# Expert weights through five buffers: three places of 96 slots, routing values in an idle buffer, buffers in address order

## The chip, the core and the metric

The kernel runs on one core of a Trainium2 chip. A core has five engines that matter here: PE (matmul; its weight loads are listed as PEld), DVE (elementwise work), ACT (activations and copies), POOL (general work) and SP, which mostly issues DMAs. Each engine works through its own list of instructions in order and waits on semaphores that others raise. Sixteen DMA engines move data between HBM and SBUF (the on-chip memory); PE writes its sums to PSUM.

The metric is the device time of one execution in microseconds, the median of several.

## The reference

Two residual layers over 256 tokens of width 1024, in float32. The first is attention of two kinds and a dense SwiGLU; the second is sliding-window attention, a short convolution and, last, eight experts of which each token takes two. Only this last part is touched:

```
logits = (xt @ w_router).astype(float32)          # 256 tokens, 8 experts
top_vals, top_idx = lax.top_k(logits, 2)
top_w = softmax(top_vals)
gates = einsum('nk,nke->ne', top_w, one_hot(top_idx, 8))
y = zeros_like(xt)
for e in range(8):
    y = y + gates[:, e:e+1] * swiglu(xt, w_gate[e], w_up[e], w_down[e])   # 1024 -> 3584 -> 1024
out = rms_norm(h + y, final_norm)
```

`top_k` prefers the smaller index where two logits are equal.

## The kernel before, in words

Up to about 500 us the kernel does everything ahead of the experts: each dense weight comes in as a load of 1 MB (`raw`), is split into a high and a low part (`whi`, `wlo`; ACT, DVE and POOL share this) and used in three products. The last of these weights is `w_out` of the second layer, four pieces: two for the first 512 columns, then two for the others. The stretch between the last pieces holds the routing: `route1` transposes h into the buffer `t.dr[0]` (tile `raw`), `logits` multiplies it with the router, `route2` and `route3` make the norm (DVE, POOL, then ACT writes the scaled `xg`), and `choose` (L929 to L956) ranks each token's eight logits, by counting for each expert how many beat it. The rank gives the mask `mb`, two products give every token's position among its expert's tokens, and `dispatch` and `gather` pick each expert's tokens by a product with a matrix of zeros and ones.

The experts are worked through in eight places. Place 0 always holds expert 0; the other seven experts are sorted by their number of tokens (`arrange`, L959 to L982), and `RANKS` says which of them goes to which place. `CAPS` is the number of slots (rows for tokens) that a place has: 64 or 96. If an expert has more tokens than its place has slots, a second pass with the weights of that expert runs after the first (`rest`, under `tc.If(t.over > 0)`). A place has twelve loads of 3,584 KB from HBM: four of w_gate, four of w_up, four of w_down (`part_in`, L1122, and `part_out`, L1130). A load of w_gate or w_up of a place with 64 slots takes two groups of column tiles on PE for each of four k (`into`, L1140), one with 96 slots three; a load of w_down takes seven steps of y, and with 96 slots seven of yo beside them (`down`, L1186). The order within a place: gate and up for the first half of the hidden units, with the last down loads of the place before between them, then gate, down of the first half, and up for the second half. Work on tokens (dispatch, gather, transposes of hid, scatter into h) is put between these by the list `fill`.

The loads go through five buffers of 28 KB per partition (`raw()`, L135), taken in turn: two from the pool `big`, which is opened early and whose two loads come in pieces during the first layer, and three from the pool `big2`, opened in `experts_open` at the start of the expert part. Its memory is what the parts of the kernel before have left; so the first load into each of the three waits for whoever used that memory last. Here the three loads are sent at once, and SP issues them in this order. From then on every `into` and `down` sends the next load when it has used its own (`weights.send()`), so a load is issued when the load five places ahead of it has been read. SP's list is in order: a load that has to wait holds up those behind it.

PE's order, and for a part of the routing ACT's and DVE's too, is the order in which the code is written (`in_order`). The rest is set by the tile framework, which also adds the waits.

The lines that matter most, in `experts_open` and in `raw`:

```
raw_pools.append((lpool("big2", 3), 3, BIG))
turn[0] = 2
for _ in range(3):
    weights.send()
```

```
n = sum(c for _, c, _ in raw_pools)
i = turn[0] % n
turn[0] += 1
```

## Time and profile before

| | us |
|---|---|
| median of 3 runs | 1336.55 |
| lowest and highest run | 1336.16, 1337.74 |
| the profiled execution | 1339.13 |
| span of the profiled execution | 1337.30 |
| PE busy in the span | 1285.7 |
| DVE, ACT, POOL busy | 373.7, 303.3, 167.3 |

The span runs from the first to the last instruction of one execution. A share of busy time is a mean over stages: up to 500 us the DMA engines move less than 300 GB/s, from 500 us on both PE and the DMA engines are shown as nearly always busy. The clock that PE was granted was 0.984 of full speed over the whole span. In the rows, "x" is a count of instructions; matmuls of float32 appear as two instructions each; a bracket at the end of a row of the timeline gives how long the engine was idle ahead of it and what ended that.

### The profile page before, as it was taken

What the parts mean: (1) busy time and instruction counts of PE and PEld (TensorE: products, weight loads), DVE (VectorE), ACT (ScalarE), POOL (GpSimd) and SP (SyncE); (2) the same over time, 40 slices, a digit from 0 to 9 for tenths busy, and PEclk for the clock granted to TensorE, in tenths of its full rate; (3) what the DMA queues carried; (4) which work ended last, traced back from release to release, by engine and by line L of the source; (5) the groups of instructions that cost most, each with busy time, mean ns of one, the idle gap of its engine ahead of it and who ended that gap; (6) DMA issues with size and microseconds to landing.
All of it is one profiled execution on the core that took longest, in us unless ns stands there. A gap on an engine that the chain in (4) does not pass through costs nothing.

```text
span 1337.3 us, 23873 instructions
## 1 busy us (share of the span) xinstructions
PE 1285.7 (96%) x10713; PEld 697.2 (52%) x10713; DVE 373.7 (28%) x697; ACT 303.3 (23%) x495; POOL 167.3 (13%) x116
## 2 busy tenths in 40 slices
PE   7999899999999999999999898999999999999995
PEld 6876678888879783433333332433333343333332
DVE  7666445445465831001012001000201200100202
ACT  6565444443344621100000100100000010000001
POOL 3311344334434110000000000000000000000000
PEclk9999899999999999999999999999999999999997
DMA  8620785555555249999999999999999999999993
GB/s 272 207 93 1 294 287 189 182 177 178 187 166 181 95 183 433 415 427 431 422 426 430 416 428 425 424 432 386 397 384 399 429 420 428 434 419 426 427 426 134
DMA packets 75758, 431.71 MB, mean 323 GB/s; under 512 B 3676, under 2 KB 7792, under 8 KB 71424
## 3 DMA queue, kind: packets, MB, share of 16 engines
q1 hardware_dynamic: 75088, 428.48, 80.0%
q8 instruction: 86, 1.41, 0.4%
q0 software_dynamic: 416, 1.10, 0.2%
q10 hardware_dynamic: 144, 0.52, 0.1%
q14 instruction: 24, 0.20, 0.0%
HBM read 429.04 MB, written 1.05 MB: 322 GB/s over the span
## 4 chain that ended last, share of the span: by engine, by line
PE 82%; DMA 11%; DVE 2%; ACT 1%; POOL 1%; issue 0%; POOLq 0%; ACTq 0%
PE mm L1150 32%; PE y L1193 11%; PE mm L201 8%; PE mm L202 8%; PE mm L203 8%; DMA big<-in_l_w_up_dram 8%; PE yo L1197 4%; DMA big<-in_l_w_down_dram 2%; PE tt L1177 1%; PE tt L1101 1%; PE ww L373 1%; PE ww L203 1%; PE ww L201 1%; PE ww L202 1%; PE mm L416 1%; DMA raw<-in_l_w_gate_dram 1%
## 5 line engine op out<-in xcount | busy, mean ns | idle before, releaser
L1150 PE MATMUL mm<-big,g 128*32 128x448 f32 x5120 | 495.1, 544 | 11.6 <-DMA big<-in_l_w_up_dram 10.5
L1150 PEld LDWEIGHTS mm<-big,g 128*32 128x32 f32 x5120 | 165.4, 111 | 320.1 <-issue 297.5
L1193 PE MATMUL y<-big,ehT 128*32 128x512 f32 x1792 | 215.2, 593 | 0.4 <-DMA big<-in_l_w_down_dram 0.4
L164 POOL TENSOR_TENSOR wlo<-raw,whi 128x288 fp32r<-128x288 f32 (+6 forms) x74 | 154.5, 2089 | 287.2 <-ACT whi L160 266.5
L162 DVE TENSOR_TENSOR wlo<-raw,whi 128x1760 fp32r<-128x1760 f32 (+6 forms) x74 | 143.0, 1934 | 134.0 <-ACT whi L160 133.7
L160 ACT ACTIVATE whi<-raw 128x2048 fp32r<-128x2048 f32 (+4 forms) x74 | 134.4, 1816 | 154.2 <-PE mm L203 82.3
L201 PE MATMUL mm<-whi,xh 128*128 128x512 f32 (+3 forms) x352 | 139.1, 396 | 1.7 <-ACT whi L160 0.9
L202 PE MATMUL mm<-wlo,xh 128*128 128x512 f32 (+3 forms) x352 | 137.2, 390 | 3.0 <-POOL wlo L164 3.0
L203 PE MATMUL mm<-whi,xl 128*128 128x512 f32 (+3 forms) x352 | 137.0, 390 | 1.4 <-DVE xl L290 1.3
L1178 ACT ACTIVATE ehT<-tt 128x512 f32<-128x512 f32 (+1 forms) x32 | 15.6, 487 | 520.3 <-PE tt L1177 520.2
L1164 DVE TENSOR_TENSOR hid<-hid,mm 128x448 f32<-128x448 f32 x40 | 24.9, 621 | 306.8 <-PE mm L1150 303.7
L1294 POOL TENSOR_TENSOR fs<-fs,nhalf 128x1 f32<-128x1 f32 x2 | 1.1, 548 | 830.3 <-DVE fs L1293 830.3
L1193 PEld LDWEIGHTS y<-big,ehT 128*32 128x32 f32 x1792 | 56.9, 110 | 81.5 <-issue 62.9
L201 PEld LDWEIGHTS mm<-whi,xh 128*128 128x128 f32 x352 | 67.7, 192 | 17.6 <-issue 1.8
L202 PEld LDWEIGHTS mm<-wlo,xh 128*128 128x128 f32 x352 | 67.7, 192 | 16.9 <-POOL wlo L164 3.3
L203 PEld LDWEIGHTS mm<-whi,xl 128*128 128x128 f32 x352 | 67.3, 191 | 16.8 <-DVE xl L290 3.1
L1197 PE MATMUL yo<-big,ehT 128*32 128x256 f32 x896 | 68.9, 379 | 0.0
L1197 PEld LDWEIGHTS yo<-big,ehT 128*32 128x32 f32 x896 | 29.1, 110 | 67.0 <-issue 65.3
L201 PE MATMUL mm<-xh,whi 128*128 128x256 f32 x160 | 46.6, 291 | 0.0
L202 PE MATMUL mm<-xl,whi 128*128 128x256 f32 x160 | 45.2, 283 | 0.0
L203 PE MATMUL mm<-xh,wlo 128*128 128x256 f32 x160 | 45.2, 283 | 0.0
L1180 DVE COPY ehT<-tt 128x384 f32<-128x384 f32 x16 | 8.9, 558 | 124.0 <-PE tt L1177 124.0
(310 smaller groups left out, 1048.0 us busy)
## 6 DMA issues: line engine op xcount, KB each, us to landing
big<-in_l_w_up_dram SPq DMA_DIRECT2D x32, 3584.0 KB, 26.8
big<-in_l_w_down_dram SPq DMA_DIRECT2D x31, 3584.0 KB, 26.2
big<-in_l_w_gate_dram SPq DMA_DIRECT2D x30, 3584.0 KB, 24.7
raw<-in_l_w_in_dram SPq DMA_DIRECT2D x15, 1024.0 KB, 5.0
raw<-in_l_w_gate_dram SPq DMA_DIRECT2D x14, 1024.0 KB, 5.0
raw<-in_l_w_up_dram SPq DMA_DIRECT2D x14, 1024.0 KB, 5.0
raw<-in_l_w_down_dram SPq DMA_DIRECT2D x14, 1024.0 KB, 4.9
raw<-in_l_w_out_dram SPq DMA_DIRECT2D x8, 1024.0 KB, 5.0
```

Source lines behind the costliest of these rows:

```text
L160: A.activation(hi, v, AF.Copy)
L162: V.tensor_tensor(lo[:, :, :m], v[:, :, :m], hi[:, :, :m].bitcast(F32), op=OP.subtract)
L164: G.tensor_tensor(lo[:, :, m:], v[:, :, m:], hi[:, :, m:].bitcast(F32), op=OP.subtract)
L201: T.matmul(ps, l[0], r[0], start=first, stop=False, **kw)
L202: T.matmul(ps, l[0], r[1], start=False, stop=False, **kw)
L203: T.matmul(ps, l[1], r[0], start=False, stop=last, **kw)
L373: T.matmul(p[:, i, Q], q[i][:, qs], k[i][:, 0:n], start=True, stop=bias is None)
L1150: T.matmul(ps[key][j][i * O:(i + 1) * O], x[:, k0 + k, g * O:(g + 1) * O], w[:, k, c:c + CH], **at)
L1164: V.tensor_tensor(x[:, g], x[:, g], ps["u"][g], op=OP.mult)
L1178: copy = V.tensor_copy if j0 else lambda a_, b_: A.activation(a_, b_, AF.Copy)
L1193: T.matmul(t.y[c * O:(c + 1) * O], x[:, (2 * i + c % 2) * O:(2 * i + c % 2 + 1) * O], w[:, j, c // 2 * 512:(c // 2 + 1) * 512], **at)
L1197: T.matmul(t.yo[c * O:(c + 1) * O], x[:, (4 + i) * O:(5 + i) * O], w[:, j, c * 256:(c + 1) * 256], **at)
```

## The change

`CAPS` and `RANKS` are changed, so that the places with 96 slots are 1, 3 and 5 in place of 1, 3, 4 and 6. The three experts with most tokens (of the seven sorted ones) get 96 slots, where four did; the fourth goes to place 2, with 64. The groups of places that are gathered together are (0), (1, 2), (3, 4), (5, 6), (7), where they were (0), (1, 2), (3), (4, 5), (6, 7).

The pool `big2` with three buffers becomes three pools `big2`, `big3`, `big4` with one buffer each, used in this order.

The small values of the routing (`lg`, `gt`, `rank`, `far`, `pos`, `count` and those of `arrange` and `gates`) move from the pool `rp` into the first 528 numbers per partition of `t.dr[0]`, the buffer that held h transposed for the router; `rp` gets smaller by as much, and the pools that are opened above it start lower.

In `choose` the two comparisons, the product with `lower` and the sum become a subtraction and one comparison with a constant `least`, which is minus the smallest normal number where the other expert has the smaller index, and zero elsewhere. `gt` is float32 now, and was bf16.

```diff
-CAPS = (64, 96, 64, 96, 96, 64, 96, 64)
-RANKS = (0, 4, 1, 2, 5, 3, 6)
+CAPS = (64, 96, 64, 96, 64, 96, 64, 64)
+RANKS = (0, 3, 1, 4, 2, 5, 6)
...
+    least = consts.tile([128, NE, NE], F32, name="least")
...
+        V.tensor_scalar(least, lower, -2.0 ** -126, None, op0=OP.mult)
...
+    def tmp(*shape):
+        n = math.prod(shape)
+        v = t.dr[0][:, t.used:t.used + n]
+        t.used += n
+        if len(shape) == 1:
+            return v
+        names = "abc"[:len(shape)]
+        return v.rearrange(f"p ({' '.join(names)}) -> p {' '.join(names)}", **dict(zip(names, shape)))
...
     def choose():
         rp = t.rp
-        t.lg = rp.tile([128, NB, NE], F32, name="lg")
+        t.used = 0
+        t.lg = tmp(NB, NE)
         V.tensor_copy(t.lg, t.pl)
-        gt = rp.tile([128, NB, NE, NE], BF, name="gt")
-        eq = rp.tile([128, NB, NE, NE], BF, name="eq")
-        t.rank = rp.tile([128, NB, NE], F32, name="rank")
+        gt = tmp(NB * NE, NE).rearrange("p (b e) f -> p b e f", b=NB)
+        t.rank = tmp(NB, NE)
...
-        V.tensor_tensor(eq, other, own, op=OP.is_equal)
-        V.tensor_tensor(gt, other, own, op=OP.is_gt)
-        V.tensor_tensor(eq, eq, lower[:, None, :, :].to_broadcast([128, NB, NE, NE]), op=OP.mult)
-        V.tensor_tensor(gt, gt, eq, op=OP.add)
+        V.tensor_tensor(gt, other, own, op=OP.subtract)
+        V.tensor_tensor(gt, gt, least[:, None, :, :].to_broadcast([128, NB, NE, NE]), op=OP.is_gt)
         V.tensor_reduce(t.rank, gt, axis=AX.X, op=OP.add)
...
-        raw_pools.append((lpool("big2", 3), 3, BIG))
+        raw_pools.extend((lpool(f"big{i}"), 1, BIG) for i in range(2, 5))
...
-    mine = experts((0,) * NE, CAPS, ((0,), (1, 2), (3,), (4, 5), (6, 7)), [do(experts_open)],
+    mine = experts((0,) * NE, CAPS, ((0,), (1, 2), (3, 4), (5, 6), (7,)), [do(experts_open)],
```

What this does to the lists of the engines, at three places.

SP, from the last load of `w_out` to the third load that waits for PE's use of a buffer. The names: `big` is an expert load, `most` the expert numbers that SP reads; a bracket lists the semaphores on which a row waits, by the engine or DMA lane that raises them. Before:

```order
L149 DMA raw<-in_l_w_out_dram 128x4x512 [waits DMAHW1_49,DVE_49,Pool_49]
L1124 DMA big<-in_l_w_up_dram 128x4x1792 [waits DVE_49,DMASW1_49,PE_49,Activation_49]
L1124 DMA big<-in_l_w_up_dram 128x4x1792 [waits DVE_49,PE_49,Pool_49]
L1124 DMA big<-in_l_w_gate_dram 128x4x1792
L1036 TENSOR_LOAD most [waits DVE_49]
L1036 ISA x2
L1124 DMA big<-in_l_w_gate_dram 128x4x1792 [waits PE_49]
```

Now:

```order
L149 DMA raw<-in_l_w_out_dram 128x4x512 [waits DMAHW1_49,DVE_49,Pool_49]
L1134 DMA big<-in_l_w_up_dram 128x4x1792 [waits DVE_49,DMASW1_49,PE_49,Activation_49]
L1134 DMA big<-in_l_w_up_dram 128x4x1792 [waits PE_49]
L1134 DMA big<-in_l_w_gate_dram 128x4x1792 [waits PE_49,Pool_49]
L1046 TENSOR_LOAD most [waits DVE_49]
L1046 ISA x2
L1134 DMA big<-in_l_w_gate_dram 128x4x1792 [waits PE_49]
```

The order is the same; the waits of the second and third of the three first loads have moved. Before, the second waits for the count that PE's last product of the fourth piece of `w_out` raises (and the split of that piece), and the third has no wait of its own. Now the second waits for the count of PE's last product of the second piece, the third for that of the third piece and POOL's part of its split. The first waits for the same as before: the last values of the convolution.

DVE, the ranks in `choose`, from the copy of the logits to the mask. Before:

```order
L932 COPY lg<-mm 128x16
L939 TENSOR_TENSOR eq<-lg 128x128
L940 TENSOR_TENSOR gt<-lg 128x128
L941 TENSOR_TENSOR eq<-eq,lower 128x128
L1005 TENSOR_REDUCE mx_4220<-lg 128x2
L942 TENSOR_TENSOR gt<-gt,eq 128x128
L943 TENSOR_REDUCE rank<-gt 128x16
L944 TENSOR_SCALAR mb<-rank 128x16
```

Now (all the routing values are in the tile `raw`):

```order
L945 COPY raw<-mm 128x16
L951 TENSOR_TENSOR raw<-raw 128x128
L1015 TENSOR_REDUCE raw<-raw 128x2
L952 TENSOR_TENSOR raw<-raw,least 128x128
L953 TENSOR_REDUCE raw<-raw 128x16
L954 TENSOR_SCALAR mb<-raw 128x16
```

Two operations on 128 elements are gone from the row ahead of the mask; nothing else has moved on DVE there.

PE, from the end of place 3 into place 4: `mm` is a gate or up product, `tt` from `disp` the gather of the next group, `tt` from `hid` a transpose; x48 is one load with 96 slots, x32 one with 64. Before:

```order
L1101 MATMUL tt<-disp,xg 128x160 x4
L1150 MATMUL mm<-big,g 32x448 x48
L1101 MATMUL tt<-disp,xg 128x160 x4
L1150 MATMUL mm<-big,g 32x448 x96
L1177 MATMUL tt<-ident,hid 128x128 x7
L1150 MATMUL mm<-big,g 32x448 x48
L1177 MATMUL tt<-ident,hid 64x128 x7
L1118 MATMUL tt<-ident,disp 96x128 x2
```

Now:

```order
L1207 MATMUL yo<-big,ehT 32x256 x4
L1160 MATMUL mm<-big,g 32x448 x128
L1187 MATMUL tt<-ident,hid 128x128 x7
L1160 MATMUL mm<-big,g 32x448 x32
L1187 MATMUL tt<-ident,hid 64x128 x7
L1128 MATMUL tt<-ident,disp 64x128 x2
```

The gather has left place 3 (x128 is two loads of place 3 and the first of place 4), and the loads of place 4 take 32 products each in place of 48.

## Rows read from the trace of the kernel before

**Rows 1.** The head of the page: the span.

```profile
span 1337.3 us, 23873 instructions
```

**Rows 2.** Places 2 to 6: length, PE, PEld, DVE, ACT, POOL busy; clock, DMA, GB/s.

```profile
681.00:776.90 95.90, 91.10 (x911) 34.72 (x903) 10.64 (x20) 9.00 (x21) 0.00 (x0) 0.98 1.01 422
776.90:898.42 121.52, 116.61 (x1171) 44.60 (x1175) 11.54 (x24) 9.67 (x23) 0.00 (x0) 0.99 1.01 428
898.42:1015.17 116.75, 115.85 (x1258) 43.80 (x1254) 12.12 (x22) 8.24 (x17) 0.00 (x0) 1.00 0.97 390
1015.17:1106.12 90.95, 90.04 (x915) 35.29 (x911) 12.07 (x26) 8.69 (x21) 0.00 (x0) 1.00 1.01 422
1106.12:1217.02 110.90, 110.53 (x1139) 39.77 (x1135) 9.65 (x16) 7.49 (x15) 0.00 (x0) 0.98 1.01 426
```

**Rows 3.** Timeline of SP's queue: issues of loads 2 and 3, 4, 5, 49, 63, 93.

```profile
469.39 24.78 SPq L1124 DMA_DIRECT2D big<-in_l_w_up_dram  x2
...
494.22 0.50 SPq L1124 DMA_DIRECT2D big<-in_l_w_gate_dram  x1
...
510.40 0.37 SPq L1124 DMA_DIRECT2D big<-in_l_w_gate_dram  x1
...
887.98 0.34 SPq L1132 DMA_DIRECT2D big<-in_l_w_down_dram  x1
...
1021.19 0.38 SPq L1124 DMA_DIRECT2D big<-in_l_w_up_dram  x1
...
1270.90 0.38 SPq L1124 DMA_DIRECT2D big<-in_l_w_up_dram  x1
```

**Rows 4.** DMA issues, last column us to landing: loads 2, 4, 5, 49, 63, 93.

```profile
big<-in_l_w_up_dram SPq DMA_DIRECT2D x1, 3584.0 KB, 12.2
...
big<-in_l_w_gate_dram SPq DMA_DIRECT2D x1, 3584.0 KB, 22.3
...
big<-in_l_w_gate_dram SPq DMA_DIRECT2D x1, 3584.0 KB, 14.6
...
big<-in_l_w_down_dram SPq DMA_DIRECT2D x1, 3584.0 KB, 19.5
...
big<-in_l_w_up_dram SPq DMA_DIRECT2D x1, 3584.0 KB, 16.2
...
big<-in_l_w_up_dram SPq DMA_DIRECT2D x1, 3584.0 KB, 28.6
```

**Rows 5.** Line 1132, the loads of w_down, all of them.

```profile
DMA to landing us min/median/max: 11.8/25.7/37.8
```

**Rows 6.** Timeline of PE: a load in place 2, and the last loads.

```profile
768.92 7.92 PE L1150 MATMUL mm<-big,g 128*32 128x448 f32 x64 [2.50 <-DMA big<-in_l_w_up_dram]
...
1299.53 6.22 PE L1150 MATMUL mm<-big,g 128*32 128x448 f32 x64 [2.40 <-DMA big<-in_l_w_up_dram]
...
1308.12 12.22 PE L1193 MATMUL y<-big,ehT 128*32 128x512 f32 x112 [0.42 <-DMA big<-in_l_w_down_dram]
```

**Rows 7.** Timeline of the routing: ranks, final gain, xg, dispatch, gather.

```profile
497.16 0.29 DVE L939 TENSOR_TENSOR eq<-lg 128x128 bf16<-128x128 f32 x1
...
497.52 0.63 POOL L1283 DMA_DIRECT2D raw<-in_final_norm_dram  x1 [6.47 <-PE mm L897]
...
497.89 0.23 DVE L942 TENSOR_TENSOR gt<-gt,eq 128x128 bf16<-128x128 bf16 x1
...
498.79 1.15 ACT L907 ACTIVATE xg<-h,rs 128x1024 f32<-128x1024 f32 x1 [2.38 <-POOL rs L906]
...
499.35 0.42 DVE L1093 TENSOR_SCALAR disp<-slot,pos 128x64 f32<-128x64 f32 x2
...
500.13 3.80 PE L1101 MATMUL tt<-disp,xg 128*128 128x64 f32 x32
```

**Rows 8.** Timeline of PE: last products of the second and third piece of w_out.

```profile
478.70 0.39 PE L203 MATMUL mm<-whi,xl 128*128 128x512 f32 x1
...
484.82 0.39 PE L203 MATMUL mm<-whi,xl 128*128 128x512 f32 x1
```

More of the change, by code (lines that the diff above doesn't have):

```diff
@@ L950, in choose @@
         T.matmul(pp[:, 16:24], onesb, mb[:, 1], start=False, stop=True)
-        far = rp.tile([128, NB, NE], F32, name="far")
+        far = tmp(NB, NE)
         V.tensor_scalar(far, mb, -1000.0, 1000.0, op0=OP.mult, op1=OP.add)
-        t.pos = rp.tile([128, NB, NE], F32, name="pos")
+        t.pos = tmp(NB, NE)
         V.tensor_tensor(t.pos, far, pp[:, 0:16].rearrange("p (b e) -> p b e", b=NB), op=OP.add)
-        t.count = rp.tile([128, NE], F32, name="count")
+        t.count = tmp(NE)
         V.tensor_copy(t.count, pp[:, 16:24])
@@ L962, in arrange @@
         c = t.count[:, 1:]
-        more, same = rp.tile(sq, F32, name="more"), rp.tile(sq, F32, name="same")
+        more, same = tmp(n, n), tmp(n, n)
         own, other = c[:, :, None].to_broadcast(sq), c[:, None, :].to_broadcast(sq)
@@ L968, in arrange @@
         V.tensor_tensor(more, more, same, op=OP.add)
-        rk = rp.tile([128, n], F32, name="rk")
+        rk = tmp(n)
         V.tensor_reduce(rk, more, axis=AX.X, op=OP.add)
-        t.at = rp.tile(sq, F32, name="at")
+        t.at = tmp(n, n)
+        t.moved = [tmp(n, n) for _ in range(2)]
         V.tensor_tensor(t.at, rk[:, None, :].to_broadcast(sq), place[:, 1, 1:, None].to_broadcast(sq), op=OP.is_equal)
@@ L985, in moved @@
         n = NE - 1
-        p = t.rp.tile([128, n, n], F32, name="moved", bufs=2)
+        p = t.moved[0]
+        t.moved.reverse()
         V.tensor_tensor(p, t.at, x[:, None, 1:].to_broadcast([128, n, n]), op=OP.mult)
@@ L998, in gates @@
         rp = t.rp
-        t.gate = gate = rp.tile([128, NB, NE], F32, name="gate")
-        tw = rp.tile([128, 4, NB], F32, name="tw")
-        oh = [rp.tile([128, NB, NE], F32, name=f"oh{i}") for i in range(2)]
-        mx = [rp.tile([128, NB], F32, name=f"mx{i}") for i in range(2)]
+        gate, tw = tmp(NB, NE), tmp(4, NB)
+        oh, mx = [tmp(NB, NE) for _ in range(2)], [tmp(NB) for _ in range(2)]
         for i in range(2):
@@ L1013, in gates @@
         V.tensor_tensor(tw[:, 3], tw[:, 1], tw[:, 2], op=OP.mult)
-        gt2 = rp.tile([128, NB, NE], F32, name="gt2")
+        gt2 = tmp(NB, NE)
         V.tensor_tensor(gate, oh[0], bc(tw[:, 2]), op=OP.mult)
```

## The prediction, made before the changed kernel was run

> **What bounds the kernel now.** I read the table of stretches first, then the timeline of SP's queue with the landing time of each load, then the timelines of the other engines where two stretches meet. The profiled execution spans 1337.3 us [rows 1]; outside the span lie 1.8 us more, and its 1339.13 us are 2.6 above the median of the three timed runs, 1336.55. All terms below are differences inside the span, and I take them off the median.
>
> From about 504 us to the end the kernel streams 96 loads of 3,584 KB through five buffers. I number them in order of use, 0 to 95 (the last is cut into three). Load n is issued when PE has read load n-5 for the last time. In the table by place [rows 2] both engines look full: PE is busy nearly all of each stretch, and the DMA engines show a share of 1.01. Which of them ends last is told by the landing times, not by the shares. Loads land in the order of issue. Load 5, issued at 510.40, lands 14.6 us later, at 525.0; load 49 (887.98 + 19.5) at 907.5; load 63 (1021.19 + 16.2) at 1037.4; load 93, the last one that feeds hid, (1270.90 + 28.6) at 1299.5 [rows 3, 4]. So 44 loads land in 382.5 us and the 30 up to load 93 in 262.1: 74 in 644.6, 8.71 us each (8.69 and 8.74 in the two parts). Between them 14 loads take 129.9 us, 9.28 each: there the stream lost 129.9 - 14 x 8.71 = 7.9 us.
>
> Why it lost them: the time from issue to landing says how much is queued ahead of a load. A load with nothing ahead takes 12.2 us (load 2, issued at 469.39 [rows 3, 4]); over the stream the time goes up to 37.8 us and down to 11.8 [rows 5]. It comes down to that floor at the end of places 3 and 4, the two neighbours of 96 slots. Place 4 is the stretch 898 to 1015: PE busy 115.85 of 116.75 us, DMA at 390 GB/s in place of 422 to 428 [rows 2]. Twelve loads at 8.71 are 104.5 us, so there PE is the late one, gives buffers back too slowly, and the queue runs dry. Everywhere else from load 3 on the stream itself is late: PE waits 4.8 us in place 2 and 4.9 in place 3 (stretch less busy time), and 2.40 us for load 93 [rows 2, 6].
>
> **The change, part by part.**
>
> *Places.* One place of 96 becomes one of 64 and no two of 96 are neighbours. A place of 96 between places of 64 costs PE what place 6 cost, 110.9 us (stretch 1106 to 1217); a place of 64 after one of 96, with the gather of the next two, what place 5 cost, 90.95 [rows 2]. Against 104.5 for the stream PE falls behind by 6.4 in the one and wins 13.5 in the other. The time to landing had gone up to 37.8 us before place 3 [rows 5] and the queue runs dry at 12.2, so some 25 us would have to be lost: a lone place of 96 never does that. The stall goes: **-7.9 us**, bounds 7.5 (at 8.74 a load) and 8.3 (at 8.69). What is late next is the stream, which ran at 8.7 before and after the stall, with times to landing from 15 to 37 us alike [rows 4, 5].
>
> *The gather of the next group* moves out of place 3 (96 slots) into places of 64. Cover: PE's waits there. Nothing.
>
> *Buffers in address order.* Before, load 2 was issued at 469.39 and load 3 only at the end of the 24.78 us that their row covers, 493.8; load 4, which waits for nothing of its own, stood behind it in SP's queue until 494.22 [rows 3]. Now load 3 waits for PE's last product of the second piece of w_out, and load 4 for that of the third (and POOL's part of the split). Those products stand at 478.70 and 484.82 [rows 8]. So load 3 leaves at about 479.5, load 4 at about 485.6; behind load 2, which lands at 481.6, they land near 492 and 500; before, load 4 landed at 516.5 (494.22 + 22.3). Behind them in SP's queue are only the read of the expert numbers, which waits for DVE's routing operations in any case, and load 5. Load 5 cannot come earlier than PE's first release, 510.40; but it finds an empty queue, and takes 12.2 us in place of 14.6: **-2.4 us**. Load 6 is issued one load of products later (6.22 us [rows 6]), before load 5 lands, so the stream is closed from there. The 2.4 us are not lost later, since PE's waits in places 2 and 3, 9.7 us together, are larger: the stream stays the late one. Bounds: 1.9 (an empty-queue load taking 12.7) to 2.8 (11.8, [rows 5]).
>
> *Ranks in two operations.* Five operations on 128 elements become three; the two that go lie at 0.23 to 0.29 us each, some 0.45 on DVE's path with the gaps between starts [rows 7]. The path to the first gather has another end, though: block 1 of xg. POOL's queue spends 497.52 to 498.15 on issuing the load of the final gain, only then raises to the power, and ACT scales xg from 498.79 to 499.94; the gather starts at 500.13 [rows 7]. The dispatch matrix is written by 499.77 (499.35 + 0.42 [rows 7]), before xg. So nearly all of the 0.45 hides behind xg; what can be won is the first two products of the gather: 0.2 us, bounds 0 and 0.45. It moves PE's first release and so load 5: **-0.2 us**.
>
> *Routing values in the buffer of h transposed.* The same operations at other addresses; each reads what DVE or ACT has just written, in the same order. The gain's load goes to the other half of that buffer. One more operation makes `least` near the kernel's start, where DVE is not the late one. Nothing.
>
> *The end.* From load 93 on nothing is changed: 1337.3 - 1299.5 = 37.8 us. But PE, with less to do in place 6, comes to load 93 having waited for each load before it. In place 2, where PE waits, the granted clock was 0.98, in place 4 1.00 [rows 2]. After a wait of 2.50 us the 64 products of a load took 7.92 us, not 6.22; after a wait of 2.40, at load 93, they took 6.22 [rows 6]. So 1.7 us are lost or not, as it falls: **+0.9**, bounds 0 and 1.7. In mid-stream the same loss costs nothing, since 7.92 is under 8.71.
>
> Sum: -7.9 - 2.4 - 0.2 + 0.9 = -9.6 us. 1336.55 - 9.6 = 1327.0.
>
> **Rivals.**
>
> *The front gives nothing* (load 5 takes 14.6 as before, for a reason that the rows don't show): 1336.55 - 7.9 + 0.9 = 1329.6. For it: one isolated load is thin evidence.
>
> *The stretch 907 to 1037 is slow for a reason of its own*, not PE's releases: then the 7.9 stay, and 1336.55 - 2.6 + 0.9 = 1334.9. Against it: the times to landing shrink to the floor exactly there.
>
> *PE falls to the lower clock and stays there.* PE now waits before almost every load of 64 slots. Were every such load read at 1.2 GHz, it would take 12.4 us (twice 6.22), PE would be late, stop waiting, and so recover: in mid-stream it limits itself. At the end there is no cover: load 93 and the last two loads at half rate cost 6.2 + 12.2 = 18.4 us more [rows 6], 1336.55 - 10.5 + 18.4 = 1344.5, slower than before. It decides if the loss after a wait is the whole load and what follows, and not 1.7 us. The rows speak for 1.7 (7.92), and the 112 products at 1308.12 ran at full rate. The Trainium skill (TensorE: Matmul & The Clock Gate, section HAM oscillation — how this bites in real kernels) says that a loop whose products are shorter than its wait for the next load drops to the lower clock at each tile; by it this rival would be the likely one, while the trace agrees in part: one drop in two waits of that length.
>
> *The smaller capacity overflows.* Counted from the reference's logits, the experts get 58, 62, 69, 65, 61, 61, 72 and 64 tokens. Place 0 (expert 0) holds 64; of the others three exceed 64, and the fourth has 64 exactly, which is what its place now holds. One token more there, from rounding, and the extra pass runs: 12 loads, 12.2 + 11 x 8.71 = 108 us, and an end of about 20 (37.8 less 2 x 8.71 in which the last two loads land): 1327 + 128 = 1455. Before, that expert had a place of 96. Against it: the nearest second and third logits lie 0.005 apart, and the kernel keeps each dense weight in a high and a low part.
>
> *The stream runs faster than counted*: its two parts differ by 0.05 us a load; 88 loads from 5 to 93 at 8.67, as far below 8.71 again, would take 3.5 us less, 1323.5. Nothing else in the rows speaks for it.
>
> **How the numbers follow.** Forecast 0.70, front gives nothing 0.10, stretch with its own reason 0.07, lower clock 0.04, overflow 0.04, a faster stream 0.05. The forecast's own bounds are 1336.55 less 7.7 to 11.55: 1325.0 to 1328.9, and 0.8 more for the spread of the timed runs. To hold 8 in 10 the range takes in the front's rival and part of the last: 1323.8 to 1330.6. A measurement of this kernel can tell about 0.2%, 2.7 us, from no change. Faster by more: 0.70 + 0.10 + 0.05 = 0.85; within: 0.07; slower: 0.08.
>
> **What would show it.** Right: loads 3 and 4 issued near 479.5 and 485.6; load 5 landing near 522.5; no time to landing under 15 us after place 1, and about 425 GB/s in every 10 us from 520 to 1290; load 93 landing near 1289; PE waiting for loads in places 4, 6 and 7. Wrong: rates under 400 GB/s anywhere in mid-stream (the stall is not PE's), a clock below full through the last 20 us of products (the clock), or a second set of 12 loads after 1320 us (overflow).

## The result, and the profile after

The changed kernel takes 1329.09 us, the median of 12 runs (1325.19 to 1334.3), beside 1337.72 for 12 runs of the kernel before (1334.62 to 1341.74): a ratio of 0.9926, 95% interval 0.991 to 0.9942, so 9.9 us off (7.8 to 12.0), where 9.6 were forecast. The two medians by themselves lie 8.6 us apart. The profiled execution spans 1328.1 us, 9.2 less than before [rows 1].

The head of the page of after, and of its GB/s row (40 equal slices of the span; the experts' loads begin to stream in slice 17):

```profile
span 1328.1 us, 22867 instructions
...
PE 1253.5 (94%) x10219; PEld 678.7 (51%) x10219; DVE 368.7 (28%) x686; ACT 300.2 (23%) x489; POOL 167.5 (13%) x116
...
GB/s 274 207 95 1 282 301 173 180 188 190 179 167 181 109 314 283 419 428 431 422 426 427 420 428 421 427 432 421 427 428 418 427 428 423 431 425 425 427 418 97
```

The table of stretches of after for places 2 to 7, the last one up to the landing of load 93 (length, then busy time of PE, PEld, DVE, ACT, POOL; clock, DMA share, GB/s); it answers [rows 2]:

```profile
680.90:773.11 92.21, 90.19 (x911) 34.93 (x903) 12.07 (x26) 8.68 (x21) 0.00 (x0) 1.00 1.01 422
773.11:887.65 114.54, 109.29 (x1139) 39.40 (x1143) 9.64 (x16) 7.49 (x15) 0.00 (x0) 1.00 1.01 427
887.65:983.51 95.86, 91.73 (x911) 35.07 (x903) 12.07 (x26) 8.68 (x21) 0.00 (x0) 0.98 1.01 425
983.51:1098.45 114.94, 111.07 (x1139) 39.80 (x1143) 9.65 (x16) 7.49 (x15) 0.00 (x0) 0.99 1.01 427
1098.45:1191.09 92.64, 89.32 (x911) 34.31 (x903) 10.60 (x20) 8.80 (x21) 0.00 (x0) 1.00 1.01 425
1191.09:1289.68 98.59, 78.31 (x696) 26.23 (x696) 7.08 (x11) 5.86 (x11) 0.00 (x0) 0.95 1.01 426
```

The 390 GB/s of place 4 are gone: every place now streams at 422 to 427, and PE has waits in each (length less busy time: 2 to 5 us, and 20 in place 7).

The timeline of SP's queue of after, issues of loads 2 and 3 (one row), 4, 5, 49, 63 and 93, as in [rows 3]:

```profile
469.80 10.81 SPq L1134 DMA_DIRECT2D big<-in_l_w_up_dram  x2
...
485.73 0.37 SPq L1134 DMA_DIRECT2D big<-in_l_w_gate_dram  x1
...
510.57 0.37 SPq L1134 DMA_DIRECT2D big<-in_l_w_gate_dram  x1
...
878.63 0.34 SPq L1142 DMA_DIRECT2D big<-in_l_w_down_dram  x1
...
993.77 0.38 SPq L1134 DMA_DIRECT2D big<-in_l_w_up_dram  x1
...
1251.98 0.38 SPq L1134 DMA_DIRECT2D big<-in_l_w_up_dram  x1
```

The DMA issues of after, us to landing, for loads 3, 4, 5, 49, 63 and 93, as in [rows 4]:

```profile
big<-in_l_w_up_dram SPq DMA_DIRECT2D x1, 3584.0 KB, 11.4
...
big<-in_l_w_gate_dram SPq DMA_DIRECT2D x1, 3584.0 KB, 14.7
...
big<-in_l_w_gate_dram SPq DMA_DIRECT2D x1, 3584.0 KB, 11.3
...
big<-in_l_w_down_dram SPq DMA_DIRECT2D x1, 3584.0 KB, 27.0
...
big<-in_l_w_up_dram SPq DMA_DIRECT2D x1, 3584.0 KB, 33.9
...
big<-in_l_w_up_dram SPq DMA_DIRECT2D x1, 3584.0 KB, 37.7
```

Load 5 lands at 510.57 + 11.3 = 521.9 (525.0 before), load 93 at 1251.98 + 37.7 = 1289.7 (1299.5 before). So the 9.2 us of the span are three pieces. Up to load 5: 3.1 less. From load 5 to load 93: 767.8 us in place of 774.5, 6.7 less. From load 93 to the end: 38.4 in place of 37.8, 0.6 more. The middle piece can be split where the prediction put the stall: load 49 lands at 905.6 and load 63 at 1027.7, so these 14 loads take 122.1 us in place of 129.9, 7.8 less. Ahead of load 49 the 44 loads take 1.3 us more than before, and behind load 63 0.2 less. From load 14 on no load takes less than 23.9 us to land: the queue never runs dry.

The timeline of PE of after, the last loads (start, us, the work, and in brackets the idle time ahead and what ended it), as in [rows 6]:

```profile
1272.09 7.91 PE L1203 MATMUL y<-big,ehT 128*32 128x512 f32 x56 [3.26 <-DMA big<-in_l_w_down_dram]
...
1280.91 6.22 PE L1160 MATMUL mm<-big,g 128*32 128x448 f32 x64 [0.91 <-DMA big<-in_l_w_up_dram]
...
1289.72 7.72 PE L1160 MATMUL mm<-big,g 128*32 128x448 f32 x64 [2.59 <-DMA big<-in_l_w_up_dram]
...
1299.70 12.22 PE L1203 MATMUL y<-big,ehT 128*32 128x512 f32 x112 [0.32 <-ACT ehT L1188]
```

The 0.6 us at the end are there: load 93's 64 products took 7.72 us behind a wait of 2.59, where before they took 6.22 behind 2.40 [rows 6]. The granted clock over these products is 0.80 in after and 1.00 in before; it is a mean of the clock's two levels, 0.5 (1.2 GHz) and 1 (2.4 GHz).

### The profile page after: what moved, and what is told of

It reads as the page before. It is cut to its first block, busy times and chain, and to the rows that moved or that the text cites. A ratio compares the mean times of both kernels' runs of the same rounds, so it can differ in the third digit from the quotient of the medians.

```text
span 1328.1 us, 22867 instructions
## 1 busy us (share of the span) xinstructions
PE 1253.5 (94%) x10219; PEld 678.7 (51%) x10219; DVE 368.7 (28%) x686; ACT 300.2 (23%) x489; POOL 167.5 (13%) x116
## 4 chain that ended last, share of the span: by engine, by line
PE 73%; DMA 19%; DVE 2%; ACT 1%; POOL 1%; issue 0%; POOLq 0%; ACTq 0%; DVEq 0%
PE mm L1160 28%; DMA big<-in_l_w_up_dram 16%; PE y L1203 8%; PE mm L201 8%; PE mm L202 8%; PE mm L203 8%; PE yo L1207 3%; DMA big<-in_l_w_gate_dram 3%; PE ww L375 1%; PE tt L1187 1%; PE ww L201 1%; PE ww L202 1%; PE ww L203 1%; PE mm L418 1%; DMA raw<-in_l_w_gate_dram 1%; PE tt L412 1%
## 5 line engine op out<-in xcount | busy, mean ns | idle before, releaser
L1160 PE MATMUL mm<-big,g 128*32 128x448 f32 x4864 | 474.6, 547 | 25.4 <-DMA big<-in_l_w_up_dram 18.2
L1160 PEld LDWEIGHTS mm<-big,g 128*32 128x32 f32 x4864 | 156.3, 111 | 324.0 <-issue 286.3
L1203 PEld LDWEIGHTS y<-big,ehT 128*32 128x32 f32 x1792 | 56.5, 110 | 104.7 <-issue 79.8
L1207 PE MATMUL yo<-big,ehT 128*32 128x256 f32 x672 | 51.7, 379 | 0.0
L1207 PEld LDWEIGHTS yo<-big,ehT 128*32 128x32 f32 x672 | 21.8, 110 | 50.3 <-issue 49.0
```

The costliest lines, as they stand in the source:

```text
L1160: T.matmul(ps[key][j][i * O:(i + 1) * O], x[:, k0 + k, g * O:(g + 1) * O], w[:, k, c:c + CH], **at)
L1203: T.matmul(t.y[c * O:(c + 1) * O], x[:, (2 * i + c % 2) * O:(2 * i + c % 2 + 1) * O], w[:, j, c // 2 * 512:(c // 2 + 1) * 512], **at)
L1207: T.matmul(t.yo[c * O:(c + 1) * O], x[:, (4 + i) * O:(5 + i) * O], w[:, j, c * 256:(c + 1) * 256], **at)
```

## The experiments

For each kernel the same three stretches were read from its profile, to some 0.1 us; "load 5" is the time from its issue to its landing. Differences in the span of one profile hold more than these: ahead of load 5 the executions differ by 3 to 4 us among themselves, whatever the kernel (see the last section).

| kernel | load 5 | load 5 to 93 | load 93 to end | time, ratio to before (95%) |
|---|---|---|---|---|
| before | 14.6 | 774.5 | 37.8 | 1 |
| after | 11.3 | 767.8 | 38.4 | 0.9926 (0.991 to 0.9942) |
| e1 places alone | 14.6 | 767.0 | 38.5 | 0.9956 (0.9937 to 0.9974) |
| e2 front alone | 11.2 | 772.8 | 37.7 | 0.9958 (0.9942 to 0.9973) |
| e3 pair | 11.3 | 772.8 | 39.3 | 0.9954 (0.9938 to 0.9971) |
| e4 three in a row | 11.5 | 789.7 | 37.2 | 1.0077 (1.0061 to 1.0094) |
| e5 order alone | 11.2 | 774.5 | 37.7 | one run, 1332.45 us |
| e6 values alone | 11.3 | 767.9 | 37.2 | one run, 1326.01 us |
| e7 all 64 | 11.2 | 765.0 | 36.8 | 0.9898 (0.9879 to 0.9916) |
| e8 filled wait | 11.3 | 768.2 | 37.6 | 0.992 (0.9905 to 0.9935) |
| e9 four operations | 11.2 | 768.1 | 36.9 | one run, 1325.53 us |
| e10 shorter front | 12.2 | 767.0 | 37.0 | one run, 1329.39 us |
| e11 halves | 9.6 | 768.3 | 35.9 | 0.9896 (0.9878 to 0.9914) |
| e12 halves, gain on ACT | 9.7 | 768.2 | 35.8 | 0.9898 (0.9881 to 0.9915) |

For e11 and e12 a load is two DMAs, and the second half is what is given.

**Places alone (e1).** On the kernel before:

```diff
-CAPS = (64, 96, 64, 96, 96, 64, 96, 64)
-RANKS = (0, 4, 1, 2, 5, 3, 6)
+CAPS = (64, 96, 64, 96, 64, 96, 64, 64)
+RANKS = (0, 3, 1, 4, 2, 5, 6)
...
-    mine = experts((0,) * NE, CAPS, ((0,), (1, 2), (3,), (4, 5), (6, 7)), [do(experts_open)],
+    mine = experts((0,) * NE, CAPS, ((0,), (1, 2), (3, 4), (5, 6), (7,)), [do(experts_open)],
```

> Kernel before with the new CAPS, RANKS and groups alone (three places of 96 slots, no two of them neighbours); buffers, routing and ranks as before. Theory A (the stall at places 3 and 4 was PE giving buffers back too slowly; the front is a separate term): loads 3 and 4 are still issued near 494, load 5 lands near 525, no time to landing falls under 20 us after place 1, and the time is 6.1 us under the kernel before (6.7 of the stream less 0.6 at the end), bounds 4.5 to 7.5. Rival B (the whole gain is the earlier start of the stream, the places only move waits about): 0 to 1.5 us under. Rival C (all of it is the places): 9 us under.

Load 5 took 14.6 us as before; the stream took 767.0 us, and places 3 and 4 ran at 427 and 424 GB/s. In time 5.9 us under before (0.9956, 3.5 to 8.4): theory A; B and C are out by the trace and by the interval.

**Front alone (e2).** The kernel after with the lines above turned back.

> Kernel after with the old CAPS, RANKS and groups: buffers in address order, routing values in the idle buffer and ranks in two operations, but four places of 96 with places 3 and 4 as neighbours. Theory A: loads 3 and 4 issued near 480 and 486, load 5 lands near 522 in place of 525.0; the stall is back, with the DMA rate under 400 GB/s in place 4 and times to landing down to about 12 us; the time is 2.5 to 3.2 us under the kernel before. Rival B (the front is the whole gain): 8 to 9 us under. Rival D (what the front wins is eaten by the stall later): 0 to 0.8 us under.

Load 5 lands 11.2 us after its issue, and the stall is back. The stretch of place 4 of e2:

```profile
893.24:1010.00 116.76, 115.86 (x1258) 43.88 (x1254) 12.12 (x22) 8.23 (x17) 0.00 (x0) 1.00 0.98 401
```

Rivals B and D are out. But the gain is more than theory A gave: 5.6 us (3.6 to 7.8). A part of the reason is in the profile: the stream lost 5.0 us against after, not 6.7. In place 3 of before PE's clock fell after a wait, here it didn't. PE's timeline at load 38, the last wait ahead of the stall, of before and then of e2:

```profile
813.06 17.31 PE L1150 MATMUL mm<-big,g 128*32 128x448 f32 x164 [3.41 <-DMA big<-in_l_w_up_dram]
```

```profile
809.58 18.25 PE L1160 MATMUL mm<-big,g 128*32 128x448 f32 x192 [2.25 <-DMA big<-in_l_w_up_dram]
```

At e2's rate (18.25 / 192) 164 products are 15.6 us: before lost 1.7 there. e5, which has the old places too, kept its clock at load 38 (18.25 us for the 192 products) and lost it at the next 96 products, 10.92 us in place of 9.23:

```profile
827.66 10.92 PE L1150 MATMUL mm<-big,g 128*32 128x448 f32 x96
```

From the landing of load 38 to the issue of load 62, at the end of place 4, 202.2 us pass in before and in e5 and 200.5 in e2. PE is the late engine all through these two places, so the 1.7 us end up in the stall whole, wherever in them they are lost.

**Two neighbours, PE's work as after (e3).**

```diff
-CAPS = (64, 96, 64, 96, 64, 96, 64, 64)
-RANKS = (0, 3, 1, 4, 2, 5, 6)
+CAPS = (64, 96, 64, 96, 96, 64, 64, 64)
+RANKS = (0, 3, 1, 2, 4, 5, 6)
```

> Kernel after, three places of 96 as in it, but at 1, 3 and 4, so that two are neighbours; PE's products are the same in number as in the kernel after, to the last one. Theory A (what counts is how far PE falls behind in a row): the stall of the kernel before comes back at the end of place 4, times to landing fall to about 12 us there, and the time is 6 to 8 us over the kernel after, so 1.5 to 3.5 us under the kernel before. Rival E (what counts is PE's work in all, one place of 96 fewer): the same as the kernel after within 1 us, some 9 us under the kernel before.

The stall is back with three places of 96 as well: times to landing fall to 12.6 us, and the stretch of place 4 reads

```profile
886.16:1008.06 121.90, 120.68 (x1290) 47.37 (x1286) 13.83 (x30) 10.32 (x25) 0.00 (x0) 1.00 0.98 403
```

The stream takes 5.0 us more than in after with the same products. That is below the 6 to 8 of theory A, and in time the two differ by less than their intervals; rival E is refused by the trace, not by the clock on the wall.

**Three neighbours, PE's work as after (e4).**

```diff
-CAPS = (64, 96, 64, 96, 64, 96, 64, 64)
-RANKS = (0, 3, 1, 4, 2, 5, 6)
+CAPS = (64, 64, 96, 96, 96, 64, 64, 64)
+RANKS = (3, 0, 1, 2, 4, 5, 6)
```

> Kernel after with the three places of 96 at 2, 3 and 4; PE's products again the same in number. Theory A, from the costs of a place in the rows: PE falls behind the stream by 6.4 us in place 2 and 12.3 in each of places 3 and 4, 31 in all, against the 25 us by which the time to landing can fall (37 to 12): the stream loses about 6 us, bounds 3 to 11, over the kernel after, all of it at the end of place 4; 0 to 6 us under the kernel before. Rival E (PE's work in all counts): the same as the kernel after within 1 us.

Now the clock on the wall tells it too: 10.3 us over the kernel before (1.0077), some 20 over after, with the same number of products. Rival E is out. Theory A has the mechanism, but its 6 us are far too few: the stream lost 21.9. The stretches of places 2 to 4 of e4:

```profile
665.52:788.39 122.87, 119.15 (x1171) 45.84 (x1175) 11.69 (x24) 9.77 (x23) 0.00 (x0) 0.97 1.01 426
788.39:905.16 116.77, 115.86 (x1258) 43.89 (x1254) 12.12 (x22) 8.24 (x17) 0.00 (x0) 1.00 0.97 397
905.16:1027.07 121.91, 120.69 (x1290) 47.46 (x1286) 13.85 (x30) 10.31 (x25) 0.00 (x0) 1.00 0.92 368
```

Twelve loads at 8.725 us (after: 767.8 / 88) are 104.7, so PE falls behind by 18.2, 12.1 and 17.2 us: 47.5, not 31. I had priced places without the gather of the next group. In place 2 of e4 that is 32 products of 192 columns, 6.3 us, and the clock stood at 0.97. The groups of PE in that stretch, the gather's row (busy us, mean ns):

```profile
L1111 PE MATMUL tt<-disp,xg 128*128 128x192 f32 x32 | 6.3, 339 | 0.0
```

With the measured lengths the sum closes to within 2 us. PE's lag over the neighbouring places, less what the time to landing can fall to its floor of 12 us, is the loss: e4 47.5 - 24.6 = 22.9 (21.9 measured); e3 28.6 - 24.7 = 3.9 (5.0); e2 27.7 - 24.7 = 3.0 (5.0); before 28.9 - 24.1 = 4.8 (6.7). This is bookkeeping after the run, with the lengths that the run had; it shows that nothing large is missing from the sum, not that the lengths could be told ahead.

**Address order alone (e5), values alone (e6).** e5 is the kernel before with the first edit below; e6 is the kernel after with the edit turned back.

```diff
-        raw_pools.append((lpool("big2", 3), 3, BIG))
+        raw_pools.extend((lpool(f"big{i}"), 1, BIG) for i in range(2, 5))
```

> Kernel before with the three buffers of one each, in address order, and nothing else. In its list load 3 waits for PE's last product of the second piece of w_out, load 4 for that of the fourth piece. Theory A (load 5 gains because the queue is empty when it is issued near 510.5; it matters little when loads 3 and 4 left, as long as both have landed by then): load 3 issued near 480, load 4 near 494, landing near 506; load 5 lands 11.3 to 12.2 us after its issue, near 522, the whole of the gain of the front by this part alone. Rival F (the address order and the moved values each bring a part): load 5 lands between 523 and 524.5.

> Kernel after with one pool of three buffers again, so without the address order; routing values in the idle buffer, ranks and places as after. In its list load 3 waits for PE's last product of the third piece, load 4 for nothing of its own. Theory A: loads 3 and 4 both issued near 486, load 4 landing near 506; load 5 lands 11.3 to 12.2 us after its issue, near 522, as in the kernel after; either part of the front does all of it. Rival F: load 5 lands between 523 and 524.5.

DMA issues of e5, loads 4 (issued at 491.07) and 5 (507.29):

```profile
big<-in_l_w_gate_dram SPq DMA_DIRECT2D x1, 3584.0 KB, 13.7
...
big<-in_l_w_gate_dram SPq DMA_DIRECT2D x1, 3584.0 KB, 11.2
```

DMA issues of e6, loads 4 (issued at 483.80, right behind load 3) and 5 (507.86):

```profile
big<-in_l_w_gate_dram SPq DMA_DIRECT2D x1, 3584.0 KB, 22.3
...
big<-in_l_w_gate_dram SPq DMA_DIRECT2D x1, 3584.0 KB, 11.3
```

In e5 load 4 lands at 504.8, in e6 at 506.1, 2.5 and 1.8 us before load 5 is issued, and in both load 5 has the whole gain. So the two edits of the front are not two gains: either gives all of it, and the second adds nothing.

**All places of 64 slots (e7).** The edit; place[:, 0], the number of slots that the test for a second pass uses, is set to 96 so that no second pass runs.

```diff
-CAPS = (64, 96, 64, 96, 64, 96, 64, 64)
+CAPS = (64, 64, 64, 64, 64, 64, 64, 64)
...
-            G.memset(place[:, 0, i:i + 1], float(CAPS[i]))
+            G.memset(place[:, 0, i:i + 1], 96.0)
```

> Kernel after with 64 slots in every place and the second pass kept off, so that the tokens beyond 64 of three experts (14 of 512 token-expert pairs) are left out. PE has some 54 us less to do than in the kernel after (three places by about 18). Theory A (from load 5 on the stream of loads sets the time and PE hides behind it): the time is that of the kernel after within 1.5 us, 7 to 11 us under the kernel before, and 88 loads from 5 to 93 take 766 to 769 us (767.8 in the kernel after). Rival G (PE's work still shows through in the places of 96): 5 to 50 us under the kernel after.

PE is busy 664.7 us from 504 us to load 93, in place of 746.3 in after. The stream takes 2.8 us less, the end 1.6 less, and the ratio is 0.9898 beside 0.9926, 3.7 us with intervals that overlap. So of 82 us of PE's busy time (54 was too low a price) at most some 4 come through: theory A for nearly all of it, but not within its 1.5 us. The 1.6 at the end are hardly PE's lighter work, since e9, with the places of after, took 36.9 there too. Six landings in e7 lie more than 9.2 us behind the one before, eight in after, at 8.6 us otherwise; that is most of the 2.8, and no run tells what makes a landing late.

**The wait before load 93 filled (e8).** Ahead of the products of load 93:

```diff
+                if (name, e, r, k0) == ("up", NE - 1, 1, 4) and isinstance(base, tuple):
+                    out_.append(do(keep, 20))
...
+        def keep(n):
+            for _ in range(n):
+                T.matmul(t.yo, onesb, onesb[:, None, :].to_broadcast([128, 2, 128]), start=True, stop=True)
```

> Kernel after with twenty small products whose result nobody reads, put in PE's order just ahead of the products of load 93, where PE waits 2.6 us and the 64 products behind it took 7.72 us in place of 6.22. Theory A (the wait costs PE its clock, and at the end nothing hides that): load 93's 64 products take 6.2 to 6.4 us, and the stretch from load 93's landing to the end falls from 38.4 to 36.9 us: 1.5 us under the kernel after, some 10 under the kernel before. Rival H (the slow products are not a matter of the wait): 7.7 us as before, no gain, or up to 1 us lost to the added products.

PE's timeline of e8 there:

```profile
1286.00 2.36 PE L1166 MATMUL yo<-onesb 128*128 128x256 bf16 x20
1288.45 6.22 PE L1160 MATMUL mm<-big,g 128*32 128x448 f32 x64
```

The products took 6.22 us, at a granted clock of 1.00: theory A at its place. The end came only 0.8 us sooner (37.6), since the scatter behind it ran slower (0.67 us for its first product, 0.50 in after), and in time nothing can be told from the kernel after. By itself this profile doesn't refuse rival H: in e6 and e9, without any filler, the products took 6.22 us too, behind waits of 2.34 and 2.56, and the end 37.2 and 36.9. What speaks for the wait is a count over the twelve profiles with whole loads, of the waits of PE ahead of 64 gate or up products in a row. All 86 waits of 0.3 to 1.9 us were followed by 6.22 us. Of the 81 waits of 2.2 us and more, 58 were followed by 7.65 to 8.6 us and 23 by 6.22. So in the stream the loss stands behind the longer waits alone, and behind these it falls or doesn't.

**Ranks in four operations (e9).** On the kernel after:

```diff
-        V.tensor_tensor(gt, other, own, op=OP.subtract)
-        V.tensor_tensor(gt, gt, least[:, None, :, :].to_broadcast([128, NB, NE, NE]), op=OP.is_gt)
+        eq = t.rp.tile([128, NB, NE, NE], F32, name="eq")
+        V.tensor_tensor(eq, other, own, op=OP.is_equal)
+        V.tensor_tensor(gt, other, own, op=OP.is_gt)
+        V.tensor_tensor(eq, eq, lower[:, None, :, :].to_broadcast([128, NB, NE, NE]), op=OP.mult)
+        V.tensor_tensor(gt, gt, eq, op=OP.add)
```

> Kernel after with the ranks in four operations again (two comparisons, a product with the index order, a sum), all else as after. From the last rs operation of DVE to the first product of the gather 3.59 us pass in the kernel after, 3.68 in the kernel before. Theory A (the two operations saved hide behind xg and PE's ten filler products): the mask is 0.3 to 0.5 us later against that operation, the gather starts 3.6 to 3.7 us after it, and load 5 is issued within 0.2 us of where it would have been. Rival I (the ranks are on the path): the gather starts 4.0 us or more after it.

PE's timeline of after (DVE's last rs operation starts at 496.88), fillers, first position product, gather:

```profile
497.21 2.06 PE L914 MATMUL ww<-onesb 128*128 128x256 bf16 x10
499.06 0.21 PE L956 MATMUL mm<-mb,strict 128*128 128x8 bf16 x1
...
500.47 3.89 PE L1111 MATMUL tt<-disp,xg 128*128 128x64 f32 x32
```

and of e9 (the operation starts at 493.94):

```profile
494.26 1.25 PE L914 MATMUL ww<-onesb 128*128 128x256 bf16 x10
496.32 0.17 PE L959 MATMUL mm<-mb,strict 128*128 128x8 bf16 x1 [0.81 <-DVE mb L957]
...
497.30 3.76 PE L1114 MATMUL tt<-disp,xg 128*128 128x64 f32 x32
```

The mask is 0.4 us later (496.08, 2.14 after the operation; 1.74 in after), but the gather starts 3.36 us after it, sooner than the 3.59 of after. The two profiles differ in more than the edit, though: the ten fillers took 2.06 us in after, at a granted clock of 0.57, and 1.25 in e9, at 1.00, and in after it is they, not the mask, that the position products stand behind. The edit is better read beside e6, which has two operations and fillers as fast as in e9 (the operation starts at 494.52):

```profile
494.85 1.25 PE L914 MATMUL ww<-onesb 128*128 128x256 bf16 x10
496.51 0.17 PE L956 MATMUL mm<-mb,strict 128*128 128x8 bf16 x1 [0.41 <-DVE mb L954]
...
497.49 0.41 PE L1111 MATMUL tt<-disp,xg 128*128 128x64 f32 x2
498.09 3.56 PE L1111 MATMUL tt<-disp,xg 128*128 128x64 f32 x30 [0.19 <-ACT xg L909]
```

Counted from the operation, e6 starts the gather at 2.97 us (e9 3.36), waits for xg in it, and ends it at 7.1 like e9: so far the two operations hide behind xg, as theory A said. But load 0's first product comes at 7.06 us in e6 and at 7.32 in e9, and load 5 is issued at 13.34 in e6 (and in e3, e4, e7 and e8) and at 13.59 in e9 (13.57 in e5, with four operations). With the slow fillers it is 13.69 with two operations (after, e2) and 13.96 and 14.01 with four (before, e1). So the two operations saved are worth about 0.25 us, a little over theory A's 0.2, and rival I is out. By what step is open: in the four kernels with four operations (and in e12, with two) PE is idle for 0.2 us just ahead of load 0's first product, and the profile names nothing that it waits for.

**A shorter front (e10), then without the cut in fillers (e12).** e10 on the kernel after:

```diff
-    plan += [do(logits, 1, 1), do(idle, 10), do(route2, 1, 1), do(route3, 1)]
+    plan += [do(logits, 1, 1), do(idle, 4), do(route2, 1, 1), do(route3, 1)]
...
-        G.dma_start(t.gfin, ...
+        nc.scalar.dma_start(t.gfin, ...
...
-    plan += [do(idle, 6)]
+    plan += [do(idle, 6), do(lambda: final_gain())]
```

> Kernel after with four filler products in place of ten between the logits and the position products, and the load of the final gain issued by ACT behind xg and no longer by POOL ahead of the power. Theory A (xg behind POOL's queue, and PE's filler products, are what the gather waits for): the gather starts 3.0 to 3.2 us after DVE's last rs operation in place of 3.59, and load 5 is issued 0.4 to 0.6 us sooner against that operation. Rival J (PE's clock falls without the filler products, and the gather and the first products pay it back): the gather starts sooner, and load 5 is issued no sooner or up to 1.5 us later.

PE's timeline of e10 (the operation starts at 493.68):

```profile
494.00 0.60 PE L914 MATMUL ww<-onesb 128*128 128x256 bf16 x4
...
496.64 7.06 PE L1111 MATMUL tt<-disp,xg 128*128 128x64 f32 x32
```

The gather starts 2.96 us after the operation, as theory A said, but it does so (2.97) in e3, e4, e6, e7 and e8 without the edit; the 3.59 of after were its slow fillers. Then it takes 7.06 us in place of 3.8, at a granted clock of 0.50; load 0's products take 7.73 for 6.22. Load 5 is issued 17.7 us after the operation, 13.7 in after: 4 us lost, more than rival J allowed. e12 has the same move of the gain, all ten fillers, and e11's halves:

> The kernel with loads in halves, with the load of the final gain issued by ACT behind xg in place of POOL ahead of the power, and with all ten filler products kept. Theory A (xg waits behind POOL's queue for some 0.6 us; the clock fell with the six filler products that were taken out, not with the earlier xg): xg starts 0.5 to 0.6 us sooner against DVE's last rs operation (1.8 in place of 2.36), the gather runs without a gap at full clock (3.6 to 3.9 us for its 32 products), and the first product of load 0 comes 6.5 to 6.8 us after that operation in place of 7.06. Rival J (an earlier gather costs the clock, whatever the fillers do): the gather takes 5 to 7 us. In time about 0.5 us under the halves by theory A, 2 to 4 over them by rival J; against the kernel before 13 to 15 us under by theory A.

There xg starts 0.87 us after the operation (2.36 in e11), the gather at 2.95 takes 3.76 at full clock, and load 0 follows 6.91 us after the operation, 7.06 in e11. So the clock went with the fillers, by these two profiles; in all thirteen profiles with ten fillers the gather takes 3.8 to 4.2 us. An xg that is 1.5 us sooner brings 0.15: the gather starts no sooner (2.95, and 2.97 in e11), since the dispatch matrix comes no sooner, and of the 0.4 us by which it ends sooner 0.2 go in idle time ahead of load 0's first product.

**Loads in halves (e11).** Every buffer as two tiles, every load as two DMAs; the core of it:

```diff
-        return pool.tile([128, size], F32, name="big")
+        return [pool.tile([128, size // 2], F32, name="big") for _ in range(2)]
...
+                for s in range(2):
+                    i0, i1 = max(i, 2 * s), min(i + n, 2 * s + 2)
+                    if i0 < i1:
+                        nc.sync.dma_start(v[s].rearrange("p (k w) -> p k w", k=2)[:, i0 - 2 * s:i1 - 2 * s],
...
-                                 w[:, k, c:c + CH], **at)
+                                 w[k // 2][:, k % 2, c:c + CH], **at)
```

> Kernel after with every buffer of 28 KB cut into two tiles of 14 KB, and every load into two DMAs, so that the first half of a load is issued when PE has read the first half of the load five ahead, and PE starts on a load when its first half has landed. PE's products are the same. Theory A (two places are still bare: the start of load 5, which waits for all 64 products of load 0 while the DMA engines have been idle since load 4 landed, and the products of load 93, which wait for all of it): the first half of load 5 is issued 3.1 us sooner and the stream starts 3.1 us earlier; behind the landing of load 93 only 32 of the 64 products are left, 3.1 us less; load for load the stream keeps 8.72 us. Together 6 us under the kernel after, bounds 4.5 to 7.5, some 15 under the kernel before. Rival K (twice as many DMAs slow the stream): 8.8 us a load or more, 88 loads 6 us slower or more, and no gain left. Rival L (the stream is not what sets the time): only the tail gains, 3 us.

DMA issues of e11, the two halves of load 5 (issued at 505.35 and 508.36, first product of load 0 at 502.08):

```profile
big<-in_l_w_gate_dram SPq DMA_DIRECT2D x1, 1792.0 KB, 8.4
...
big<-in_l_w_gate_dram SPq DMA_DIRECT2D x1, 1792.0 KB, 9.6
```

PE's timeline of e11, load 93's second half and the last loads:

```profile
1286.38 3.21 PE L1167 MATMUL mm<-big,g 128*32 128x448 f32 x32 [1.18 <-DMA big<-in_l_w_up_dram]
...
1291.86 6.70 PE L1213 MATMUL y<-big,ehT 128*32 128x512 f32 x56 [0.32 <-ACT ehT L1195]
1299.18 6.22 PE L1213 MATMUL y<-big,ehT 128*32 128x512 f32 x56 [0.63 <-DMA big<-in_l_w_down_dram]
```

e11 is the fastest here together with e12: 0.9896 of before (11.5 to 16.3 us less), 0.003 below after's ratio, some 4 us, with intervals that just overlap. The mechanism is theory A's, its 6 us are too many. The stream keeps its pace (768.3), which refuses rival K. It starts 2.8 us sooner (load 9 lands 50.6 us after the first product of load 0, 53.4 in after), which refuses rival L. The end is 2.5 us shorter and not 3.1: PE now waits 0.63 us for the first part of load 95, so that the last loads, not load 93's products, are what ends it.

## Why the prediction was right, and where not

*What bounds the kernel.* Right: PE's work in all hardly matters (e7), how far PE falls behind in a row does (e3, e4).

*Places, -7.9 (7.5 to 8.3).* The stall went as forecast: 7.8 us between loads 49 and 63. The stream's 88 loads in all took only 6.7 us less in after (7.5 in e1), because of the 1.3 us ahead of load 49 (see the address order). A step that was off: "in mid-stream the same loss costs nothing, since 7.92 is under 8.71". That holds for 64 products of a load in a place of 64. In a run of places where PE is late a clock loss adds in full, and 1.7 of the old stall was such a loss (e2 beside before and e5). And the lag of 12.3 us that e4's expectation put in for a place beside another came from a place without a gather; with one it is 17 (e4).

*The gather, moved for nothing.* Right by the sum: places 2 and 4 of after, which hold it, still have 2.0 and 4.1 us of waits.

*Address order, -2.4 (1.9 to 2.8).* Load 5 took 11.3 us, where 12.2 was put in: -3.3 in time to landing. It was issued 0.2 us later than before, since the routing of that execution came 0.4 us later. The step "the 2.4 us are not lost later" holds only in part: load 6 lands 9.5 to 10.0 us behind load 5 in every kernel with whole loads whose load 5 took 11.2 to 11.5 us, and 8.8 to 9.0 us behind it in before, e1 and e10. Ahead of load 49 after has four such late landings and before three, and that is the 1.3 us. So of the 3.1 us gained at load 5 some 2 are left; what makes a landing late is not shown. Loads 3 and 4 were issued at 480.24 and 485.73, as foreseen (479.5 and 485.6). What I hadn't seen is that the moved values alone give the same (e6): they lower the pools above them, so that even without the address order the second of the three loads waits for the third piece of w_out and no longer for the fourth.

*Ranks, -0.2 (0 to 0.45).* About -0.25 (e9 beside e6). The reason given, that the rest hides behind xg, holds for the gather, whose end does not move; that the gain would lie in the gather's first two products does not, since it shows ahead of load 0. In after PE's fillers were late as well, by their lower clock.

*The end, +0.9 (0 to 1.7).* +0.6. That the loss belongs to the wait is borne out by the count at e8, not by e8 alone.

*The sum.* -9.6 forecast, -9.2 in the spans of the two profiles. It is this near in part by luck, since the stream's 6.7 for 7.9 and the front's 3.1 for 2.6 make up for each other in part. The 1329.09 us themselves lie in the range, but 0.2 above the forecast's own 1328.9; the kernel before took 1.2 us more in these runs than the 1336.55 that the sum started from.

*Rivals.* "The front gives nothing" (1329.6) is as near to the measured time as the forecast is; it fell with the landing of load 5 in after, e2, e5 and e6, not by the time. "A reason of its own at 907 to 1037" fell with e1. Of the lower clock that stays: PE waited before many loads and lost 1.4 to 2.4 us behind some of these waits and nothing behind others, and came back within the load each time; in e7, where it waits most, the granted clock of a place was 0.93 to 0.97, and the time was the lowest of the kernels with whole loads. So the drop of which the Trainium skill (TensorE: Matmul & The Clock Gate, section HAM oscillation — how this bites in real kernels) speaks is in the traces, behind some waits and not at each load. The prediction called this rival the likely one by that section, but its case is a loop whose products are shorter than its wait; here 64 products take 6.22 us and the longest wait ahead of a load's 64 products is 4.1. In these traces the drop has a price only where no load hides it: ahead of the routing (1.5 us, see the last section), at the gather (e10: 4 us), in the places ahead of a stall (1.7 us) and at load 93. No second pass ran.

## What to carry to other kernels

With a stream through a few buffers, read from the time to landing whether the stream or the reader is late, and price a run of heavy stages as one sum: their lag together, with all that is put between them, less what the queue holds. Spread heavy stages so that the sum never exceeds it; what is then left lies where the stream starts and ends, and there smaller pieces helped (e11: some 4 us, with intervals that just overlap). Before two single profiles are compared, look whether PE's clock was the same in both: here that alone moved the start of the stream by 1.9 us. Two edits that remove the same wait are worth one of them.

## What the runs showed of the hardware

- The spread of the timed runs (1325 to 1334 us for one kernel) has a visible part in PE's clock. Behind a wait of 1.48 us at about 464, from the transposes there to the eighth product of w_out, 5.7 us pass in the profiles of before, after, e1 and e2 (products of 0.63 us each; granted clock 0.72 in before) and 4.2 in the ten others (0.39; 1.00 in e6): 1.5 us, ahead of the routing, where no load hides it. In the same four profiles the ten fillers take 2.0 to 2.2 us in place of 1.25, and load 5 is issued 0.35 us later for it (13.69 and 13.34 after DVE's operation). The prediction's two profiles, before and after, are both of this kind, so that their difference is free of it; the lower times of the single runs of e6 and e9 are not.
- The same wait has both outcomes: load 93's 64 products took 6.22 us behind 2.40 us (before) and behind 2.34 (e6), 7.72 behind 2.59 (after).
- From 520 us to 1290 the core read 422 to 428 GB/s in the places of before and after that did not stall, with all loads landing in the order of their issue. The Trainium skill (DMA: Bandwidth & Descriptors, section Where 436 GB/s comes from) says that for HBM to SBUF the HBM side binds, at some 358 GB/s, and calls its own 425 GB/s for 16 MB near the rate of the fabric; for this program, on one core, the measurement is 18 to 20% above the 358 and agrees with the 425.
- A load of 3,584 KB into an empty queue took 11.2 to 12.2 us, one of 1,792 KB 7.4 to 8.5, while in a full queue they land 8.6 and 4.3 us apart, but for about one whole load in eleven (9.3 to 10.3).
